# A decoder trunk on one core: new durations in the table that sets the order of the instructions

## The chip, the cores and the metric

The kernel runs on 1 core of one Trainium2 chip. The metric is the device time of one execution, in microseconds (us). TensorE does the matmuls, VectorE and ScalarE the elementwise work, GpSimd (POOL) a few small operations, and SyncE issues the loads.

## The reference

Two decoder layers are run over 256 positions of width 1024, in float32 (norms, convolutions, the mLSTM recurrence and the softmax are left out here):

```python
for layer in range(2):
    u = rmsnorm(h) @ w_in[layer]
    y = concat([mlstm(u), conv31(u), diff_attention(u)])
    h = h + y @ w_out[layer]
    c = rmsnorm(h)
    if layer % 2 == 0:
        f = (silu(c @ wg) * (c @ wu)) @ wd              # dense, 2816 wide
    else:                                               # top 2 of 8 experts, 3584 wide each
        f = sum(combine[:, e:e + 1] * ((silu(c @ wg[e]) * (c @ wu[e])) @ wd[e]) for e in range(8))
    h = h + f
    h = h + sigmoid(rmsnorm(h) @ w_gate[layer]) * (p[layer] @ w_ple[layer])
```

## The kernel before

**Weights.** Nearly all the time goes to weights that are used once. They come as tiles of 128x2048 float32, 1 MB each, into `raw` buffers (five of `rawp`, and in the expert stage four of `rawb`). ScalarE rounds a tile to fp32r as `hi` (`high`, L352), VectorE computes `lo = raw - hi` (`low`, L370), and TensorE multiplies by hi and by lo into the same PSUM tile. There are 4 hi and 3 lo buffers in the expert stage; both come free when TensorE has finished the tile (`done`, L397), the raw buffer when lo is made. So the hi of a tile waits for TensorE to be done with the tile four before it, and the lo for the tile three before it.

**Stages.** In each layer the in-projection goes by columns (pz, pm, pq, pk, pmv, pav), with the mLSTM, the convolution (z, on VectorE) and the attention (plg, ac, pya) beside it; then come the out-projection (pwo), the feed-forward part, and the gated input embedding (ppp, pgt). Layer 0 has the dense feed-forward part (pg, pu, pdn), layer 1 the experts.

**Experts.** They are taken in the pairs (0,1), (2,3), (4,5), (6,7), after the tokens that each expert got are gathered (pgx, gx) into slots: 128 ("many") for experts 0, 2 and 4, and 64 ("few") for the others. A tile of a many expert is 12 matmuls with 512 columns, one of a few expert 8, since hi and lo then share a pass and a small matmul `pht` folds them. Each expert has 7 slices f; a slice is two tiles gate (pmg), two up (pmu), two down (pmy). ScalarE and VectorE make from pmg and pmu the input of down: msl, msg, `pht` on TensorE, then mt in hi and lo form. The regular cycle of a pair is 12 tiles: pmg and pmu of the many expert, pmy of the few one, pmg and pmu of the few one, pmy of the many one. Between pairs results are scattered back (psc, added to h by VectorE) and the next tokens gathered. At the first slice of expert 2 `gate_up` (L1399) has a branch on the device at L1420, for experts with more than 64 tokens; it isn't taken here, but all engines meet at it.

**The order.** The kernel is written as one main stream (TensorE's matmuls) and side streams (generators, `side`). While the program is built, a planner keeps an estimated clock for each engine: `tick` adds an operation's estimated cost, `estimate` gives the time at which a stream's next step could begin, `best` (L205) takes the earliest, and `slot` (L212) writes what begins before TensorE's clock runs out, ahead of the next matmul group. hi and lo are such steps too, which `Feed.due` offers when a load's estimated landing (`pump`) and a buffer's release permit. What is written is the order on each engine. The costs are in `pe_cost` (L107), `act_cost` (L116), `dve_cost` (L123), `pool_cost` and in `pump` (L323). Every instruction goes through the helper `call`, so in the trace nearly all have its line, L101, and are told apart by the names of their tiles.

Of the kernel before, what the change touches and what calls it, by code (L numbers as in the profile page):

```python
# [64 lines left out]
def tile_trunk(ctx, tc, x, par, con, abias, wif, rw, pt, w1, w2, wgu, wdn, wpg, wpp, wm, gb, out):  # L65
# [38 lines left out]
    def size(*aps):  # L104
        return max(math.prod(a.shape[1:]) for a in aps if hasattr(a, "shape"))

    def pe_cost(op, a, kw):  # L107
        if op == "transpose":
            return 0.107
        if kw["rhs"].dtype == F32R:  # L110
            return size(kw["rhs"]) / 2400
        return max(size(kw["rhs"]) / 600, 0.1)

    tables = [None]

    def act_cost(op, a, kw):  # L116
        c = 0.2 + size(*a[:2]) / 1400
        if len(a) > 2 and a[2] not in (AF.Copy, AF.Square, AF.Abs) and a[2] != tables[0]:
            tables[0] = a[2]
            c += 1.28  # L120
        return c

    def dve_cost(op, a, kw):  # L123
        return (0.13 if op == "scalar_tensor_tensor" else 0.1) + size(*a[:2]) / 960

    def pool_cost(op, a, kw):
        return 0.25 if op in ("memset", "affine_select") else 0.13 + 0.166 * size(a[0])

    pe, act = Engine(nc.tensor, pe_cost), Engine(nc.scalar, act_cost)
    dve, pool = Engine(nc.vector, dve_cost), Engine(nc.gpsimd, pool_cost)  # L130
    main = Stream()
    cur = [main]
# [167 lines left out]
    class Feed:  # L300
# [14 lines left out]
        def pump(self, upto=None):  # L315
            while self.loaded < (upto or (len(seq) if self.order else first_moe)):
                which = next((w for w in "pb" if self.free[w]), None)
                if which is None:
                    return
                src = seq[self.loaded]  # L320
                if isinstance(src, tuple):
                    src = wm[(self.order[src[0]],) + src[1:]]
                self.dma = max(self.dma, self.free[which].pop(0)) + 2.65  # L323
                raw = (rawp if which == "p" else F[which]).tile([128, 2048], F32, name="raw" + which, tag="raw" + which)

                step = 1024 if self.loaded in (0, 1, first_moe, first_moe + 1, last_moe, last_moe + 1) else 2048
                for c in range(0, 2048, step):
                    nc.sync.dma_start(raw[:, c:c + step], src[:, c:c + step])
                self.raws[self.loaded] = raw, which, [self.dma + 2.0 - 1.3 * (1 - q) * (step == 1024) for q in range(2)]
                self.loaded += 1  # L330
# [1254 lines left out]
    for n in range(3 * DEPTH):  # L1585
        L, c = divmod(n, 3)
# [134 lines left out]
```

## Time and profile before

| | |
|---|---|
| three runs, us | 1435.37, 1439.47, 1432.83; median 1435.37 |
| profiled execution, us | 1433.88, span 1432.2, mean granted clock 0.986 |
| TensorE busy, us | 1379.7 (96%), 6500 instructions |
| VectorE busy, us | 1197.2 (84%), 1222 |
| ScalarE busy, us | 1045.5 (73%), 1194 |
| GpSimd busy, us | 58.2 (4%), 73 |
| HBM read | 435.39 MB, 305 GB/s over the span |

A trace is read by stage here: 0 to 345 us is layer 0 (its dense part from about 160 to 320), 345 to 513 attention and the rest of layer 1's mixing, 513 to 1388 the experts, and the end is the last scatter and the embedding. Matmuls overlap by their pipeline, so a duration in a row is longer than the distance of two starts. In a timeline row the time in brackets is what the engine stood idle just before, with what ended it.

### The profile page before, as it was taken

How to read it: one execution, taken by the hardware profiler on the slowest of the kernel's cores; microseconds unless marked ns; L12 is line 12 of the kernel's file. 1: busy time of each engine (PE TensorE's matmuls, PEld its weight loads, DVE VectorE, ACT ScalarE, POOL GpSimd, SP SyncE). 2: the span in 40 equal slices, each digit the busy share in tenths (PEclk: the TensorE clock that was granted, in tenths of full speed). 3: DMA queues.
4: the chain of work that ended last, by engine and by line, in shares of the span. 5: the costliest groups of instructions: out<-in, count | busy, mean ns of one | idle time of the engine just before them, and what ended most of it. 6: DMA issues, size and time to landing. Idle time of an engine off the chain costs nothing. (4 is left out here: it accounts for less than half of the span.)

```text
span 1432.2 us, 18251 instructions
## 1 busy us (share of the span) xinstructions
PE 1379.7 (96%) x6500; PEld 1118.2 (78%) x6500; DVE 1197.2 (84%) x1222; ACT 1045.5 (73%) x1194; POOL 58.2 (4%) x73
## 2 busy tenths in 40 slices
PE   7999999999999989999999999999999999999998
PEld 6777888888877867888878888887878887767666
DVE  5997654546899579999979999988999998999986
ACT  7766534436776577888878888886888888888875
POOL 0212000000031100000000000000000000000000
PEclk9998999999998989999999999999999999999999
DMA  9243555554440099999998999998999999999970
GB/s 361 89 147 126 206 176 195 187 183 170 145 147 30 16 402 421 420 422 420 421 417 337 420 407 417 406 388 319 413 415 408 402 402 367 418 420 422 421 310 30
DMA packets 62766, 437.66 MB, mean 306 GB/s; under 512 B 7120, under 2 KB 8016, under 8 KB 10832
## 3 DMA queue, kind: packets, MB, share of 16 engines
q1 hardware_dynamic: 62352, 435.42, 76.3%
q8 instruction: 52, 0.85, 0.2%
q0 software_dynamic: 320, 1.05, 0.2%
q14 instruction: 42, 0.34, 0.1%
HBM read 435.39 MB, written 1.05 MB: 305 GB/s over the span
## 5 line engine op out<-in xcount | busy, mean ns | idle before, releaser
L101 DVE TENSOR_TENSOR lo<-rawp,hi 128x2048 fp32r<-128x2048 f32 (+1 forms) x336 | 598.1, 1806 | 126.7 <-ACT hi L101 114.1
L101 ACT ACTIVATE hi<-rawp 128x2048 fp32r<-128x2048 f32 (+1 forms) x336 | 502.5, 1525 | 164.7 <-PE pg L101 34.9
L101 DVE TENSOR_TENSOR lo<-rawb,hi 128x2048 fp32r<-128x2048 f32 (+1 forms) x154 | 342.2, 2246 | 15.6 <-ACT hi L101 6.4
L101 ACT ACTIVATE hi<-rawb 128x2048 fp32r<-128x2048 f32 (+1 forms) x154 | 287.0, 1882 | 33.5 <-PE pmu L101 12.8
L101 PE MATMUL pmy<-hi,mt 128*128 128x512 f32 x616 | 224.1, 398 | 0.1
L101 PE MATMUL pmg<-hi,gx 128*128 128x512 f32 x616 | 220.8, 397 | 0.9 <-DVEq L1420 0.9
L101 PE MATMUL pmu<-hi,gx 128*128 128x512 f32 x616 | 219.3, 395 | 0.0
L101 PE MATMUL pmu<-lo,gx 128*128 128x512 f32 x448 | 177.6, 396 | 11.2 <-DVE lo L101 10.3
L101 PE MATMUL pmg<-lo,gx 128*128 128x512 f32 x448 | 177.4, 396 | 9.9 <-DVE lo L101 9.8
L101 PE MATMUL pmy<-lo,mt 128*128 128x512 f32 x448 | 175.6, 392 | 0.5 <-DVE lo L101 0.3
L101 PEld LDWEIGHTS pmg<-hi,gx 128*128 128x128 f32 x616 | 116.1, 189 | 25.2 <-issue 2.2
L101 PEld LDWEIGHTS pmy<-hi,mt 128*128 128x128 f32 x616 | 115.8, 188 | 23.7 <-DVE mt L101 0.7
L101 PEld LDWEIGHTS pmu<-hi,gx 128*128 128x128 f32 x616 | 115.8, 188 | 22.8 <-issue 0.2
L101 PEld LDWEIGHTS pmu<-lo,gx 128*128 128x128 f32 x448 | 84.1, 188 | 37.9 <-DVE lo L101 21.1
L101 PEld LDWEIGHTS pmg<-lo,gx 128*128 128x128 f32 x448 | 84.4, 188 | 35.1 <-DVE lo L101 18.4
L101 PEld LDWEIGHTS pmy<-lo,mt 128*128 128x128 f32 x448 | 84.2, 188 | 19.7 <-DVE lo L101 1.8
L101 PEld LDWEIGHTS pht<-conT,msg 128*128 128x128 f32 x560 | 73.0, 191 | 8.1 <-ACT msg L101 2.4
L101 PE MATMUL pht<-conT,msg 128*128 128x64 f32 x560 | 70.2, 268 | 1.5 <-ACT msg L101 1.5
L101 DVE SCALAR_TENSOR_TENSOR z<-zpad,parT,z 128x256 f32<-128x256 f32 x120 | 50.9, 479 | 0.3
L101 PE MATMUL pg<-hi,nh 128*128 128x512 f32 x96 | 37.7, 393 | 0.0
L101 PE MATMUL pg<-hi,nl 128*128 128x512 f32 x96 | 37.4, 390 | 0.0
L101 PE MATMUL pg<-lo,nh 128*128 128x512 f32 x96 | 37.4, 389 | 0.0
(299 smaller groups left out, 1873.0 us busy)
## 6 DMA issues: line engine op xcount, KB each, us to landing
rawp<-in_wm SPq DMA_DIRECT2D x184, 1024.0 KB, 8.7
rawb<-in_wm SPq DMA_DIRECT2D x148, 1024.0 KB, 8.7
rawp<-in_w SPq DMA_DIRECT2D x30, 1024.0 KB, 4.7
rawp<-in_wgu SPq DMA_DIRECT2D x22, 1024.0 KB, 4.7
rawp<-in_wdn SPq DMA_DIRECT2D x11, 1024.0 KB, 4.8
rawp<-in_wpg SPq DMA_DIRECT2D x5, 1024.0 KB, 4.7
rawp<-in_wm SPq DMA_DIRECT2D x8, 512.0 KB, 7.8
rawb<-in_wpg SPq DMA_DIRECT2D x3, 1024.0 KB, 10.3
```

The lines of the kernel that those rows point to most:

```text
L101: return fn(*args, **kw)
```

## The change

The figures for the duration of an instruction and of a load are others. A matmul with 512 columns has 0.228 us instead of 0.213; a hi of 2048 elements 1.836 instead of 1.663; a lo of 2048 2.203 instead of 2.233; a 64-column fold (`pht`) 0.2 instead of 0.107; a load of 1 MB 2.48 instead of 2.65. What is computed, the buffers and the order of the loads stay; the order in which ScalarE's, VectorE's, TensorE's and GpSimd's work is written moves.

```diff
@@ -108,20 +108,20 @@
         if op == "transpose":
             return 0.107
         if kw["rhs"].dtype == F32R:
-            return size(kw["rhs"]) / 2400
-        return max(size(kw["rhs"]) / 600, 0.1)
+            return 0.01 + size(kw["rhs"]) / 2350
+        return max(size(kw["rhs"]) / 600, 0.2 if size(kw["rhs"]) == 64 else 0.1)
 
     tables = [None]
 
     def act_cost(op, a, kw):
-        c = 0.2 + size(*a[:2]) / 1400
+        c = 0.1 + size(*a[:2]) / 1180
...
     def dve_cost(op, a, kw):
-        return (0.13 if op == "scalar_tensor_tensor" else 0.1) + size(*a[:2]) / 960
+        return (0.15 if op == "scalar_tensor_tensor" else 0.07) + size(*a[:2]) / 960
...
@@ -320,7 +320,7 @@
-                self.dma = max(self.dma, self.free[which].pop(0)) + 2.65
+                self.dma = max(self.dma, self.free[which].pop(0)) + 2.48
```

In the regular cycle, here of experts 2 and 3, ScalarE (its own queue, in order) has before:

```order
L101 ACTIVATE msl<-pmg 128x512
L101 ACTIVATE hi<-rawp 128x2048 x2
L101 ACTIVATE hi<-rawb 128x2048
L101 ACTIVATE mt<-pht 128x4x128
L101 ACTIVATE hi<-rawb 128x2048 x2
L101 ACTIVATE msg<-pmg 128x512
L101 ACTIVATE hi<-rawb 128x2048
L101 ACTIVATE msl<-pht 128x256
L101 ACTIVATE hi<-rawp 128x2048
L101 ACTIVATE msg<-pmu 128x512
```

and now:

```order
L101 ACTIVATE msl<-pmg 128x512
L101 ACTIVATE hi<-rawp 128x2048 x4
L101 ACTIVATE mt<-pht 128x4x128
L101 ACTIVATE hi<-rawb 128x2048 x2
L101 ACTIVATE msg<-pmg 128x512
L101 ACTIVATE hi<-rawb 128x2048 x2
L101 ACTIVATE msl<-pht 128x256
L101 ACTIVATE msg<-pmu 128x512
L101 ACTIVATE hi<-rawp 128x2048
L101 ACTIVATE mt<-msl 128x4x64
```

mt<-pht (the hi form of the many expert's down input) stands behind four hi instead of three, and msg<-pmu directly behind msl<-pht.

VectorE in the regular cycle, here of experts 0 and 1, has before:

```order
L101 TENSOR_TENSOR msl<-msl,pmu 128x512
L101 TENSOR_TENSOR lo<-rawb,hi 128x2048 x3
L101 TENSOR_TENSOR mt<-pht,mt 128x4x128
L101 TENSOR_TENSOR lo<-rawb,hi 128x2048
L101 TENSOR_TENSOR lo<-rawp,hi 128x2048 x2
L101 TENSOR_TENSOR msl<-msl,pht 128x256
L101 TENSOR_TENSOR lo<-rawp,hi 128x2048
L101 TENSOR_TENSOR mt<-msl,mt 128x4x64
```

and now:

```order
L101 TENSOR_TENSOR msl<-msl,pmu 128x512
L101 TENSOR_TENSOR lo<-rawb,hi 128x2048 x2
L101 TENSOR_TENSOR mt<-pht,mt 128x4x128
L101 TENSOR_TENSOR lo<-rawb,hi 128x2048 x2
L101 TENSOR_TENSOR lo<-rawp,hi 128x2048 x2
L101 TENSOR_TENSOR msl<-msl,pht 128x256
L101 TENSOR_TENSOR lo<-rawp,hi 128x2048
L101 TENSOR_TENSOR mt<-msl,mt 128x4x64
```

mt<-pht,mt (its lo form) stands behind two lo instead of three.

In experts 6 and 7, where both have 64 slots and a half cycle is six tiles, ScalarE has before:

```order
L101 ACTIVATE mt<-msl 128x4x64
L101 ACTIVATE hi<-rawp 128x2048 x3
L101 ACTIVATE msg<-pmg 128x512
L101 ACTIVATE hi<-rawb 128x2048
L101 ACTIVATE msl<-pht 128x256
L101 ACTIVATE hi<-rawb 128x2048
L101 ACTIVATE msg<-pmu 128x512
L101 ACTIVATE hi<-rawb 128x2048
L101 ACTIVATE mt<-msl 128x4x64
```

and now:

```order
L101 ACTIVATE msg<-pmg 128x512
L101 ACTIVATE hi<-rawb 128x2048 x2
L101 ACTIVATE msl<-pht 128x256
L101 ACTIVATE msg<-pmu 128x512
L101 ACTIVATE hi<-rawp 128x2048 x3
L101 ACTIVATE mt<-msl 128x4x64
L101 ACTIVATE hi<-rawp 128x2048
```

Two hi stand between msg<-pmg and msl<-pht instead of one, and three, instead of one, between msg<-pmu and the mt behind it.

At the branch of L1420 VectorE's last two lo before it move from ahead of the four h<-h,psc additions to behind them, still ahead of the branch, and TensorE's psc stands ahead of the last 24 pmu matmuls instead of behind them. In the attention stages VectorE's z steps move earlier, and the norm of the queries (yn) comes behind two hi halves of its weights.

## Rows read from the trace of the kernel before

**Rows 1.** The page: span, busy time of each engine, TensorE's busy tenths in forty slices.
```profile
span 1432.2 us, 18251 instructions
PE 1379.7 (96%) x6500; PEld 1118.2 (78%) x6500; DVE 1197.2 (84%) x1222; ACT 1045.5 (73%) x1194; POOL 58.2 (4%) x73
...
PE   7999999999999989999999999999999999999998
```

**Rows 2.** Windows: stretch, length, busy us (instructions) of PE, PEld, DVE, ACT, POOL; clock, DMA share, GB/s.
```profile
540.00:700.00 160.00, 160.00 (x755) 133.43 (x755) 154.32 (x89) 131.67 (x96) 0.00 (x0) 1.00 1.01 421
1240.00:1370.00 130.00, 120.18 (x566) 92.99 (x565) 124.32 (x72) 111.75 (x90) 0.00 (x0) 1.00 1.01 421
```

**Rows 3.** Timeline, TensorE, experts 0 and 1: first pmu matmul, five cycles apart.
```profile
550.97 0.39 PE L101 MATMUL pmu<-hi,gx 128*128 128x512 f32 x1
...
698.82 0.39 PE L101 MATMUL pmu<-hi,gx 128*128 128x512 f32 x1
```

**Rows 4.** The chain of waits, later pairs: start, length, engine, tile, count.
```profile
771.90 5.44 PE pmu L101 x24
...
892.85 5.44 PE pmu L101 x24
923.64 5.44 PE pmu L101 x24
...
996.25 5.44 PE pmu L101 x24
...
1148.54 5.44 PE pmu L101 x24
```

**Rows 5.** Timeline of one cycle of experts 2 and 3: ScalarE, VectorE, TensorE.
```profile
871.61 0.60 ACT L101 ACTIVATE mt<-pht 128x512 fp32r<-128x512 f32 x1 [2.15 <-PE pht L101]
872.11 3.71 ACT L101 ACTIVATE hi<-rawp 128x2048 fp32r<-128x2048 f32 x2
...
874.05 4.49 DVE L101 TENSOR_TENSOR lo<-rawp,hi 128x2048 fp32r<-128x2048 f32 x2 [0.81 <-ACT hi L101]
...
876.39 0.50 PE L101 MATMUL pmu<-lo,gx 128*128 128x512 f32 x1 [0.94 <-DVE lo L101]
```

**Rows 6.** Timeline of one cycle of experts 0 and 1: VectorE, and one TensorE row.
```profile
615.58 2.29 DVE L101 TENSOR_TENSOR lo<-rawp,hi 128x2048 fp32r<-128x2048 f32 x1 [0.43 <-PE pmu L101]
...
618.38 6.69 DVE L101 TENSOR_TENSOR lo<-rawb,hi 128x2048 fp32r<-128x2048 f32 x3
...
623.27 0.39 PE L101 MATMUL pmu<-hi,gx 128*128 128x512 f32 x1
...
624.99 0.69 DVE L101 TENSOR_TENSOR mt<-pht,mt 128x512 fp32r<-128x512 f32 x1
625.59 2.28 DVE L101 TENSOR_TENSOR lo<-rawb,hi 128x2048 fp32r<-128x2048 f32 x1
```

**Rows 7.** Timeline around the branch.
```profile
750.25 0.69 DVE L101 TENSOR_TENSOR h<-h,psc 128x512 f32<-128x512 f32 x1 [1.03 <-PE psc L101]
...
751.15 0.47 PE L101 MATMUL pmg<-hi,gx 128*128 128x512 f32 x1 [0.93 <-DVEq L1420]
```

**Rows 8.** VectorE's waits, 1240 to 1370 (total us, times, longest), and the timeline there.
```profile
DVE lo L101 <- ACT hi L101: 4.9, 9, 0.7
...
1310.05 0.42 DVE L101 TENSOR_TENSOR msl<-msl,pht 128x256 f32<-128x256 f32 x1
...
1320.23 0.38 ACT L101 ACTIVATE msl<-pht 128x256 f32<-128x256 f32 x1 [0.62 <-PE pht L101]
...
1324.82 0.42 DVE L101 TENSOR_TENSOR msl<-msl,pht 128x256 f32<-128x256 f32 x1
```

**Rows 9.** Windows (columns as rows 2) in the attention stages of layer 0 and layer 1.
```profile
98.00:104.00 6.00, 4.05 (x21) 2.70 (x19) 5.83 (x16) 5.17 (x18) 0.00 (x0) 1.00 0.23 61
106.00:114.00 8.00, 8.00 (x26) 6.24 (x25) 7.27 (x25) 5.96 (x26) 0.80 (x1) 0.50 0.09 35
450.00:462.00 12.00, 12.00 (x37) 9.27 (x38) 10.97 (x37) 8.57 (x35) 1.49 (x2) 0.50 0.00 0
```

## Prediction

> **What bounds the kernel now.** First I read the page's shares and its forty slices [rows 1]. TensorE is busy for 96% of the span, and its digit is 9 in nearly every slice, so only a moment in which TensorE waits, or runs at a lower clock, can be won or lost: 1432.2 less 1379.7 is 52.5 us in all. VectorE at 84% is next. The dense feed-forward part (160 to 320 us, the fifth to eighth slice and half of the ninth) has nothing but 9, and its order is the same before and after, so nothing happens there.
>
> A share of the whole span does not say which engine ends last in a stage, so I read windows of the expert stage [rows 2]. In experts 0 and 1 (540 to 700) TensorE works 160.00 of 160 us, with VectorE at 154.32 and the loads at 421 GB/s, a share of 1.01: all three are full, and TensorE ends last. In experts 6, 7 (1240 to 1370) TensorE loses 9.82 of 130 us, and VectorE is the fuller one, at 124.32.
>
> Then I measured the cycle of the expert loop. One cycle of a pair is twelve 1 MB weight tiles, and the first matmul of the same pmu tile marks its start. Five cycles of pair 0, 1 run from 550.97 to 698.82 [rows 3]: 147.85 us, or 29.57 each. The chain of waits marks the same point in the later pairs [rows 4]: 771.90 to 923.64 is 151.74 for five, with 30.79 for the last, and 996.25 to 1148.54 is 152.29. Twelve tiles are 12.58 MB, which at 421 GB/s take 29.89 us, so the loads pace nearly the same cycle.
>
> The 1.2 us by which the slow cycle is longer show in the timeline [rows 5]. ScalarE stands 2.15 us at mt<-pht, which TensorE has not yet produced, with two hi halves queued behind it; so VectorE waits 0.81 for a hi, and TensorE 0.94 for the lo made from it.
>
> **The change, part by part.** It removes and adds no operation, buffer or load. It changes what the planner believes, and so which instruction it writes next. The new figures are those of the rows: 24 matmuls in 5.44 us are 0.227 each [rows 4], for which the planner now has 0.228 instead of 0.213; three lo in 6.69 are about 2.20 each [rows 6], for which it has 2.20 instead of 2.23; two hi in 3.71 are about 1.85 [rows 5], for which it has 1.84 instead of 1.66. That the change does nothing can be left out, as the order of three engines differs. The load order on SyncE's queue is the same; a load waits for the lo that frees its buffer, and a lo that comes 0.6 later is hidden by the backlog of loads (share 1.01 in [rows 2]). Without the backlog it would cost up to those 0.6 per cycle.
>
> *Regular cycle, ScalarE.* mt<-pht moves behind four hi instead of two or three. One more hi, 1.85 us, then fills the 2.15 that ScalarE waited [rows 5], and the hi behind mt are one fewer. At most 0.3 of the wait is left there, and the two waits that came from it go. What is late next is on VectorE.
>
> *Regular cycle, VectorE.* Its mt<-pht,mt moves one lo forward. In the old order the three lo run from 618.38 to 625.07, with mt behind them [rows 6]. The new order puts mt, which costs 0.60 to the next start (624.99 to 625.59), ahead of the third, which then ends at about 625.67. TensorE needs it after eight hi matmuls and one more: 623.27 + 9 x 0.227 = 625.31. It would wait 0.36, and with the hand-over I take 0.4 per cycle; the bounds are 0 (an earlier start of the lo, since VectorE has two waits of 0.43 before them) and 0.6. The cycle becomes 29.57 + 0.40 = 29.97 in all pairs, just over the loads' 29.89. Experts 0, 1: 6 x 0.40 = **+2.4**. Experts 2, 3: 151.74 and a sixth cycle of 30.79, less 6 x 29.97 = **-2.7**. Experts 4, 5: 152.29 + 30.79 - 179.82 = **-3.2** (rounded).
>
> *The branch at L1420.* Before, VectorE makes the last addition of psc to h from 750.25, 0.03 after TensorE's last matmul, and TensorE goes on at 751.15, a wait of 0.93 [rows 7]. Now VectorE has two lo behind the h additions and ahead of the branch, and the last needs a buffer that TensorE frees with its last matmul before the branch. One lo of 2.2 and the 0.2 around it then stand where 0.93 stood: +1.5 (bounds 0 and 2.4). Behind the branch ScalarE has a hi ahead of a msg that TensorE's fold needs. A hi is 1.85 us [rows 5]; I take about half, +1.0 (bounds 0 and 1.85). Together **+2.5**.
>
> *Experts 6, 7.* Six tiles take 14.77 us, from the msl at 1310.05 to the one at 1324.82 [rows 8]. VectorE loses 4.9 us in 9 waits for a hi, 0.54 each, because ScalarE waits 0.62 at msl<-pht with a hi behind it. In the new order two hi come before msl<-pht and three behind msg<-pmu, and I find no place where a hi is late: I take 4.5 of the 4.9: **-4.5** (bounds 0 and -6, with the 9.82 that TensorE loses in the window above it).
>
> *Attention and convolution, both layers.* VectorE's z steps move earlier, and a norm there comes behind two hi halves. No row of before shows that order. The nearest rows are the stretches at half clock: 8 us and 12 us at 0.50 [rows 9], which in layer 0 follow a stretch where TensorE had worked only 4.05 of 6.00 us with VectorE full (5.83). If they went, half of 20 us is won (-10); if they came again with the idle time of 1.95 ahead of each, +14 is lost. VectorE's chain gets no shorter, so I stay near zero on the late side, as a few halves moved ahead cost part of one idle time: **+1.5**.
>
> The sum is 2.4 - 2.7 - 3.2 + 2.5 - 4.5 + 1.5 = -4.0, and against the profiled execution's own 1433.9 that gives 1429.9, told as **1430**. That execution is 1.5 us below the median of the runs shown (1435.4), so the new median may stand up to 1.5 higher.
>
> **The rivals.**
> *The lo is in time.* If the two waits of 0.43 in VectorE's row [rows 6] move with the order, the third lo is ready at 625.3 and the cycle stays at 29.57 in all three pairs. 18 cycles x 0.4 are 7.2 less: **1423**. For it: only 0.36 us is missing. Against it: those waits are for buffers that TensorE frees, and TensorE moves with them.
>
> *The loads set experts 6, 7.* Six tiles are 6.29 MB, 14.94 us at 421 GB/s [rows 2], and the cycle now takes 14.77. If the loaded tiles ahead are used up, nothing is left of the 4.5: **1434**. For it: a share of 1.01 through the whole window. Against it: the cycle already beats 14.94, and what VectorE waits for there is ScalarE's hi, behind a wait for TensorE.
> The Trainium skill, Perfetto Trace Analysis (section Roofline), puts the practical ceiling of a single active core at about 435 GB/s. By that figure six tiles need an estimated 14.46 us, and some 0.3 of each 0.54 would be left; the 421 of the window lies below it, and no run here shows more.
>
> *The half clock lasts longer, the slower end.* One mechanism in one place, between the in-projection and pwo: if VectorE's norm for the queries ends later, TensorE idles longer there, and the stretch at 0.50 comes a second time. Each stage pays the idle 1.95 and half of 8 or 12 us: 6 and 8 us [rows 9]. In one stage that gives about 1436, in both 1429.9 - 1.5 + 14 = 1442.4, and on the scale of the median **1443**. It decides if TensorE stands idle there once more, as it did ahead of the stretch of before. For it: that order changes most, and TensorE is idle there already. Against it: TensorE has pieces of pwo and norms to put there, and most z steps move ahead of time, not behind.
> The Trainium skill's TensorE: Matmul & The Clock Gate, Part 1, says that the clock is halved after TensorE has been little busy and restored once it works. The rows agree, with 1.00 in the idle stretch, 0.50 in the busy one that follows. By that rule the loss is several times the idle time itself.
>
> **How the numbers follow.** About 0.5%, here 7 us, is what a measurement of this kernel can tell from no change. The forecast has 0.45, and its own range is 1426 to 1435 from the bounds of the lo, the branch and experts 6, 7; about 0.14 of it lies under 1428. The lo in time has 0.25, the loads 0.13. The half clock has 0.17, of which 0.06 in one stage, and 0.11 in both. Faster by over 0.5% is then 0.25 + 0.14 = 0.39; slower 0.11, with 0.01 for the far end of the one-stage case: 0.12; the rest, 0.49, lies between. The range of 1420 to 1441 leaves out the both-stage case and the fast end of the first rival, where experts 6, 7 give 6 instead of 4.5.
>
> **What would show each step right or wrong.** Right: in experts 2 to 5 no wait of ScalarE at mt<-pht; a wait of TensorE of about 0.4 per cycle for the lo behind VectorE's mt, and 29.97 us between pmu starts, in experts 0, 1 too; TensorE 2 to 3 us idle at the branch; six tiles in about 14.2 in experts 6, 7 with no wait of VectorE for a hi. Wrong: cycles still over 30.5 (another wait has replaced the first); 14.9 in experts 6, 7 with waits for a raw tile (the loads); a granted clock of 0.50 for more than 20 us in the two stages. The forecast is wrong as a whole if the expert stage is not 6 to 10 us shorter while the mixing stages stay within 3 us.

## The result, and the profile after

The changed kernel takes 1442.06 us (median of 16 runs, 1439.65 to 1446.15), the kernel before 1434.32 (16 runs): a ratio of 1.0051, 95% interval 1.0043 to 1.0060. It is 8 us slower; 1430 was forecast, and the range ended at 1441. The profiled execution took 1442.0 us.

The page of the changed kernel, its first part and the slices, to be read beside [rows 1]:

```profile
span 1440.3 us, 18380 instructions
PE 1386.9 (96%) x6500; PEld 1123.4 (78%) x6500; DVE 1195.0 (83%) x1222; ACT 1047.0 (73%) x1194; POOL 52.9 (4%) x73
...
PE   7999999999999989999999999999999999999988
```

Nothing in it tells where the 8 us went: the shares are the same to a percent. The first pgx of each pair of experts (the gather) is a mark that both traces have. From such marks, in one profiled execution of each kernel:

| stretch | before, us | after, us | difference | forecast |
|---|---|---|---|---|
| start to first pgx (dense layer, both attentions, router) | 501.24 | 511.04 | +9.8 | +1.5 |
| experts 0, 1 | 219.60 | 222.85 | +3.3 | +2.4 |
| experts 2, 3, with the branch | 225.14 | 227.50 | +2.4 | -0.2 |
| experts 4, 5 | 224.88 | 221.97 | -2.9 | -3.2 |
| experts 6, 7 and the end | 261.3 | 256.9 | -4.4 | -4.5 |

**The expert loop did what was worked out.** Rows of the changed kernel's timeline, VectorE, ScalarE and TensorE in one cycle of experts 4 and 5, which answer to [rows 5, 6]:

```profile
1048.88 0.68 DVE L101 TENSOR_TENSOR msl<-msl,pmu 128x512 f32<-128x512 f32 x1
...
1052.28 0.57 ACT L101 ACTIVATE mt<-pht 128x512 fp32r<-128x512 f32 x1
...
1053.88 0.68 DVE L101 TENSOR_TENSOR mt<-pht,mt 128x512 fp32r<-128x512 f32 x1
...
1056.82 0.50 PE L101 MATMUL pmu<-lo,gx 128*128 128x512 f32 x1 [0.25 <-DVE lo L101]
...
1078.96 0.68 DVE L101 TENSOR_TENSOR msl<-msl,pmu 128x512 f32<-128x512 f32 x1
```

ScalarE's wait of 2.15 at mt<-pht is gone. VectorE's mt is ahead of the third lo, TensorE waits for it, and the cycle is 30.08 us from msl to msl: slower than the 29.57 of [rows 3], faster than the 30.79 of [rows 4]. It is 30.1 in all three pairs; 29.97 was forecast. Five cycles of experts 0 and 1 are 2.6 us longer than before (150.48 and 147.85, from msl to msl). What is left of the table's +3.3 lies ahead of the first of them (+0.8), where the changed kernel has a stretch at a mean clock of 0.57 (544 to 548), behind a wait of 1.24 us for a lo; the execution of before has 1.00 at that place.

In experts 6 and 7 six tiles take 13.88 us instead of the 14.77 of [rows 8], VectorE waiting for no hi. The timeline has VectorE's msl of two half cycles:

```profile
1279.45 0.41 DVE L101 TENSOR_TENSOR msl<-msl,pht 128x256 f32<-128x256 f32 x1
...
1293.33 0.41 DVE L101 TENSOR_TENSOR msl<-msl,pht 128x256 f32<-128x256 f32 x1
```

ScalarE's waits (total us, times, longest) from 1345 to 1395 us:

```profile
ACT hi L101 <- DMA rawp<-in_wm: 2.9, 5, 0.8
ACT hi L101 <- DMA rawb<-in_wm: 2.2, 5, 0.6
```

13.88 is less than the 14.94 that six tiles take to load at 421 GB/s. The tiles loaded ahead are used up, and at the end ScalarE waits for loads; the last three half cycles take 14.31, 16.12 and 11.84 us. In the second of them TensorE waits 1.70 us for a msg (at 1371.9), and the clock is at 0.50 from 1374 to 1376. Six half cycles in a row had won 5.4 us (88.72 before, 83.27 after); the stretch as a whole won 4.4.

**The branch** cost more than the 2.5 forecast: from the last msl<-msl,pmu of experts 0 and 1 to the second one of experts 2 and 3 it is 72.92 us before and 77.14 after, +4.2. The timeline there, beside [rows 7]:

```profile
760.41 2.29 DVE L101 TENSOR_TENSOR lo<-rawb,hi 128x2048 fp32r<-128x2048 f32 x1 [1.88 <-PE pmu L101]
...
763.13 2.29 DVE L101 TENSOR_TENSOR lo<-rawp,hi 128x2048 fp32r<-128x2048 f32 x1 [0.43 <-PE pmu L101]
...
765.62 0.52 PE L101 MATMUL pmg<-hi,gx 128*128 128x512 f32 x1 [2.36 <-DVEq L1420]
```

Two windows behind it (columns as rows 2), and one of TensorE's waits, for the msg of a fold:

```profile
766.00:768.00 2.00, 2.00 (x6) 1.60 (x5) 0.00 (x0) 0.17 (x1) 0.00 (x0) 0.50 0.98 385
768.00:770.00 2.00, 2.00 (x7) 1.56 (x6) 0.78 (x1) 1.21 (x1) 0.00 (x0) 0.67 0.82 340
```

```profile
PE pht L101 <- ACT msg L101: 1.2, 1, 1.2
```

The idle time is 2.36, as worked out (0.93 and 1.5), and the wait behind the branch 1.2 (1.0). What was left out is the clock: right after the idle time it is at 0.50, the 1.2 GHz level, for 2 us and part of the next two, which costs about 1.6.

**The 9.8 us ahead of the experts** are the surprise. Windows of both kernels between the same marks (columns as rows 2): in-projection from pm to pav, attention from pav to pg (layer 0) or to the router's prl (layer 1), router from prl up to the first expert matmul. First before:

```profile
25.07:80.70 55.63, 55.54 (x271) 43.92 (x270) 50.97 (x100) 39.39 (x61) 11.46 (x12) 1.00 0.44 165
80.70:142.21 61.51, 56.89 (x274) 45.10 (x272) 50.39 (x125) 42.74 (x114) 10.60 (x11) 0.92 0.36 130
359.19:427.94 68.75, 68.69 (x328) 54.83 (x327) 61.22 (x120) 49.08 (x82) 12.95 (x18) 0.98 0.42 148
427.94:489.94 62.00, 59.21 (x277) 46.76 (x276) 46.58 (x119) 40.08 (x113) 11.03 (x12) 0.89 0.09 31
489.94:512.97 23.03, 17.85 (x126) 16.89 (x125) 12.62 (x41) 10.30 (x23) 0.93 (x1) 0.80 0.49 185
```

and after:

```profile
25.57:82.37 56.80, 55.52 (x271) 43.86 (x270) 53.04 (x105) 39.67 (x61) 11.79 (x12) 1.00 0.44 162
82.37:147.06 64.69, 58.40 (x274) 45.46 (x272) 49.48 (x123) 43.69 (x115) 8.01 (x11) 0.92 0.35 123
364.37:434.21 69.84, 68.61 (x327) 54.74 (x326) 63.44 (x125) 49.34 (x82) 13.30 (x18) 0.98 0.41 145
434.21:498.19 63.98, 58.75 (x277) 45.97 (x276) 44.62 (x113) 39.82 (x113) 8.41 (x12) 0.92 0.09 30
498.19:523.05 24.86, 19.68 (x126) 18.71 (x125) 12.61 (x41) 10.41 (x23) 0.94 (x1) 0.74 0.47 178
```

TensorE's number of instructions is the same but for one, the length is not: +1.2, +3.2, +1.1, +2.0, +1.8. Length less PE's busy time gives the idle time: in the four stretches ahead of the router it grows by 1.2, 1.7, 1.2 and 2.4, in all 6.5 us. The clock is not the cause in the attentions (0.92 and 0.92; 0.89 and 0.92). In the router it is, where the clock falls from 0.80 to 0.74 and the idle time stays at 5.18: there is a new stretch at 0.50 from 500 us, while TensorE works. (Up to pgx the router takes 12.8 us instead of 11.3. The rest of the 9.8 is 0.5 us ahead of the first pm and 0.3 between the attention of layer 0 and the in-projection of layer 1.)

Where TensorE's idle time in the attention goes, by its waits (total us, times, longest): in each layer of the changed kernel, and before in layer 0 and in layer 1.

```profile
PE pat L101 <- DVE ac L101: 3.4, 3, 2.6
```

```profile
PE pat L101 <- DVE ac L101: 1.9, 2, 1.0
...
PE pat L101 <- DVE ac L101: 0.8, 1, 0.8
```

These waits grow by 1.5 and 2.6 us. ac is the product of one head's softmax chain: plg on TensorE, lg and nm on VectorE, the exponentials on ScalarE, ac on VectorE, pat on TensorE. Its start, layer 0, before:

```profile
85.59 0.92 PE L101 MATMUL plg<-kT,qT 64*128 64x256 f32 x4
86.43 2.89 PE L101 MATMUL pnd<-v,wt 128*128 128x65 f32 x24
...
91.36 1.01 DVE L101 TENSOR_REDUCE nm<-lg 128x2 f32<-128x512 f32 x2
```

and after:

```profile
87.16 2.79 PE L101 MATMUL pnd<-v,wt 128*128 128x65 f32 x24
89.88 1.57 PE L101 MATMUL plg<-kT,qT 64*128 64x256 f32 x8
...
95.67 1.01 DVE L101 TENSOR_REDUCE nm<-lg 128x2 f32<-128x512 f32 x2
...
107.14 0.90 PE L101 MATMUL pat<-conT,ac 128*128 128x128 f32 x3 [2.60 <-DVE ac L101]
```

The first plg has lost its place ahead of the 24 pnd (the mLSTM's read-out). Counted from the first pav (80.70 and 82.37), it starts at 7.5 instead of 4.9 us, and the first nm at 13.3 instead of 10.7: the chain starts 2.6 us late. The same two lines are swapped in layer 1.

### The profile page after: what moved, and what is told of

The parts are those of the page before. It is cut to its first block, busy times and chain, and to the rows that moved or that the text cites. A ratio compares the mean times of both kernels' runs of the same rounds, so it can differ in the third digit from the quotient of the medians.

```text
span 1440.3 us, 18380 instructions
## 1 busy us (share of the span) xinstructions
PE 1386.9 (96%) x6500; PEld 1123.4 (78%) x6500; DVE 1195.0 (83%) x1222; ACT 1047.0 (73%) x1194; POOL 52.9 (4%) x73
## 5 line engine op out<-in xcount | busy, mean ns | idle before, releaser
L101 PE MATMUL pmy<-hi,mt 128*128 128x512 f32 x616 | 227.1, 402 | 1.3 <-DVE mt L101 1.3
```

The costliest lines, as they stand in the source:

```text
L101: return fn(*args, **kw)
```

## The experiments

All are compared with the kernel before, run on the same chip; a ratio has its 95% interval.

**e1 and e2: the change by stages.** The old and the new figures stand side by side, and a flag is turned over where the experts begin, in `moe`, ahead of `gather(0)`. e2 begins with True and turns to False.

```diff
+    shown = [False]
...
-        c = 0.2 + size(*a[:2]) / 1400
+        c = 0.1 + size(*a[:2]) / 1180 if shown[0] else 0.2 + size(*a[:2]) / 1400
...
         emitted(("order",))
+        shown[0] = True
```

> New durations from the first gather of the experts on, old ones before it. Theory S (the loss lies in the order of attention, convolution and router, which came out 9.8 us later, while the experts' order gains about 1.7 net): mixing as before, about 1432.5 us, ratio 0.997 to 1.000. Rival W (the experts' new order is only good or bad together with the state in which the mixing leaves queues and loads): 1438 or more.

> The reverse: new durations up to the router, old ones from the first gather on. Theory S: about 1444 us (1434.3 + 9.8), the first msl of the experts 10 us later than before. Rival W: 1434 to 1438, since the old order of the experts would take up part of the delay in its waits.

e1: 1432.21 us, ratio 0.9982 (0.9971 to 0.9993). e2: 1446.55, ratio 1.0080 (1.0067 to 1.0094). Theory S holds: the experts' new order alone is a small gain, the order ahead of them a loss of 11.8 us, more than the change as a whole.

**e3: truer prices of small operations.**

```diff
-        c = 0.1 + size(*a[:2]) / 1180
+        c = 0.1 + size(*a[:2]) / 1180 + (0.18 if "accum_out" in kw else 0.0)
...
-        return (0.15 if op == "scalar_tensor_tensor" else 0.07) + size(*a[:2]) / 960
+        return max(0.2, (0.15 if op == "scalar_tensor_tensor" else 0.07) + size(*a[:2]) / 960)
```

> The new durations, and two more taken from the trace: ScalarE operations that also accumulate a sum cost 0.18 us more (0.50 and 0.38 in the trace for 256 and 128 elements, 0.32 and 0.21 in the changed table), and no VectorE operation costs less than 0.2 (the table has 0.07 for two elements). Theory P (the attention order is bad because the changed table prices its small operations lower still than the old one, away from the trace): the mixing stages come back to within 2 us of before, total about 1434. Rival C (the planner's order reacts to any figure, and a truer price does not bring a better order): the mixing stages stay 5 us or more behind those of before, total 1439 or more.

1445.75 us, ratio 1.0070 (1.0057 to 1.0083). Theory P falls: with figures nearer to the trace the kernel is 11.0 us slower than before. In its profiled execution, the slowest of the five (1450.35), the attentions take 66.1 and 69.3 us (before 61.5 and 62.0), and in layer 0 TensorE waits 6.6 us at once for ac:

```profile
PE pat L101 <- DVE ac L101: 6.6, 1, 6.6
```

**e5, e6, e7: one figure at a time, up to the router.** The flag of e2, with only ScalarE's, only VectorE's or only TensorE's new figure behind it.

> Before, with ScalarE's new durations alone, and only up to the router. Theory A (the loss comes with ScalarE's figure, which prices 256 and 128 elements lower while they take longer in the trace): at least 6 us behind before at the first gather, about 1441 or more. Rival C (no one figure carries it; any change of a figure gives another order of the attention, as good or bad as it falls): a shift of the mixing stages between 0 and 10 us for each of the three figures, none of them near 0 by itself while the others carry all.

> The same with VectorE's new durations alone, up to the router. Theory A: within 2 us of before (1434.8). Rival C: 3 us or more late.

> The same with TensorE's new pace for fp32r matmuls alone (0.228 instead of 0.213 for 512 columns), up to the router. Theory A: within 2 us of before, since that figure agrees with the trace. Rival C: 3 us or more late.

e5: 1432.84 us, ratio 0.9988 (0.9973 to 1.0003); e6: 1433.21, 0.9990 (0.9977 to 1.0002); e7: 1437.94, 1.0020 (1.0008 to 1.0033). Theory A falls. None carries the loss, and their sum, -1.8 - 1.4 + 3.3, is about nothing, where all new figures together cost 11.8 (e2; the figures of the small fold and of a load, which e2 has too, were not tried apart). Rival C as I had written it doesn't hold either: two of the three are near nothing.

What the slow kernels share was then looked for in TensorE's order. In the changed kernel, e2 and e3 the first plg stands behind pnd; before, and in e5, e6 and e7, ahead of it. It turns round when TensorE's and ScalarE's figures are new together, and not with TensorE's and VectorE's.

**e9, e10: two pairs of figures**, by the same flag.

> Before, with TensorE's and ScalarE's new durations together, only up to the router. In this order, as in the changed kernel's, TensorE's first plg of each layer stands behind the 24 pnd instead of ahead of them. Theory N (this place costs the loss: the attention's chain of dependent work starts 2.6 us later in each layer): at least 5 us over before, about 1440 or more, although the two figures alone gave -1.8 and +3.3. Rival C (orders differ at random, and the effects of the figures add up): 1436, +1.5.

> The same with TensorE's and VectorE's new durations. Here the first plg stays ahead of pnd in both layers. Theory N: within 4 us of before, under 1439. Rival C by sums: +1.9, about 1436.5; a loss of more than 5 would speak against theory N.

e9: 1444.83 us, ratio 1.0075 (1.0057 to 1.0092), 10.4 over before where the two figures alone add up to 1.5: as theory N has it. e10: 1439.66, 1.0038 (1.0019 to 1.0057), 5.2 over before. That misses the expectation (under 4) and is over the 5 that was to speak against theory N, though the interval, 2.7 to 8.2 us, leaves both open. In its profiled execution the attentions are 1.4 us longer than before, the rest is in-projection and router. The place of plg is thus not the whole loss.

**e11: that place set back.** In e2's kernel, the first head gets a rank ahead of pnd's (which has -0.5):

```diff
-        side(*[attn(hd) for hd in range(4)], pen=-0.3)
+        side(attn(0), pen=-0.6)
+        side(*[attn(hd) for hd in range(1, 4)], pen=-0.3)
```

> All new durations up to the router and old ones behind it (1446.6 measured), and the first head's attention stream is given a priority ahead of pnd's, so that the first plg stands ahead of pnd again. Theory N: the attention stages come back by 2 to 3 us per layer, about 1441. Rival C: the order behind that place differs anyway, and nothing is won: 1445 to 1448.

1439.88 us, ratio 1.0038 (1.0025 to 1.0050): 6.7 less than e2 (6.0 by the two ratios, as they ran on different chips), somewhat more than theory N has. In its timeline the first plg is 4.9 us behind the first pav again, and nm 10.1, with the same table and the same work:

```profile
88.46 0.92 PE L101 MATMUL plg<-kT,qT 64*128 64x256 f32 x4
89.30 2.89 PE L101 MATMUL pnd<-v,wt 128*128 128x65 f32 x24
...
93.67 1.01 DVE L101 TENSOR_REDUCE nm<-lg 128x2 f32<-128x512 f32 x2
```

The profiled execution shows where: the two attentions are 2.9 us shorter than e2's, and the router 1.6, since the half clock did not come there. But it is not TensorE's waiting that went. The two attentions (columns as rows 2), first of e2:

```profile
82.10:146.84 64.74, 58.45 (x274) 45.45 (x272) 49.48 (x123) 43.68 (x115) 8.01 (x11) 0.92 0.34 124
433.98:497.93 63.95, 58.71 (x277) 45.97 (x276) 44.63 (x113) 39.83 (x113) 8.42 (x12) 0.92 0.09 30
```

and of e11:

```profile
83.59:147.16 63.57, 57.32 (x274) 44.43 (x272) 49.51 (x123) 44.05 (x115) 9.76 (x11) 0.89 0.35 125
433.03:495.26 62.23, 55.77 (x277) 42.87 (x276) 44.44 (x113) 39.98 (x113) 10.16 (x12) 0.95 0.09 31
```

TensorE's busy time falls by 4.1 us, and its idle time grows by 1.2; its waits at pat for ac are 5.8 us instead of 6.8, with 3.0 new ones at plg for lg. The two attentions together (first pav to pg, and to prl), by one profiled execution of each:

| first plg | kernel | sum of both, us | TensorE idle in it, us |
|---|---|---|---|
| ahead of pnd | before; e5; e6; e7; e10; e11 | 123.5; 121.7; 122.1; 125.3; 124.9; 125.8 | 7.4; 6.8; 9.8; 13.7; 15.4; 12.7 |
| behind pnd | after; e2; e9; e3 | 128.7; 128.7; 128.8; 135.4 | 11.5; 11.5; 12.6; 18.0 |

In the sums the two groups don't overlap, though 4 us lie within the first between kernels that differ only in the order behind that place. In the idle time they do: e7, e10 and e11, with plg ahead of pnd, wait as long as the changed kernel or longer. Theory N holds for the time in e9 and e11 and misses it in e10, and its mechanism, that TensorE waits because the chain starts late, is not shown: in e10, with the first nm at 10.5 us as early as before, the waits at pat for ac are 6.6 us, in the changed kernel 6.8. Why the busy time is less with plg ahead was not separated. In e7 and e10 the clock has a part in it (0.94 over both attentions, in the changed kernel 0.92); in e11 it is 0.92 as well.

**e4: the branch.** In the changed kernel, psc of experts 0 and 1 waits for a name that is set when the last pmu ahead of the branch is written.

```diff
-                yield when(pe, *[(a, e) for a in ("Y", "PT") for e in es])
+                yield when(pe, *[(a, e) for a in ("Y", "PT") for e in es], *(["GO"] if es == [0, 1] else []))
...
             if (e, f) == (2, 0):
+                set_ready("GO")
```

> The changed kernel, but the scatter of experts 0 and 1 is held until the last pmu before the branch is written, so that psc covers VectorE's two lo again. Theory B (at the branch the change costs 1.4 of idle time, about 1.6 by the half clock after it and 1.2 by TensorE's wait for a msg): the wait for the branch is 0.9 instead of 2.4, no stretch at 0.50 near it, about 1438 us, 4 less than the changed kernel. Rival I (the idle time alone counts; the clock falls there anyway): 1.5 less, about 1440.5.

1438.97 us, ratio 1.0027 (1.0017 to 1.0037), 3.1 less than the changed kernel (3.4 by the two ratios): between the two theories, nearer to B. TensorE's wait is the old one, and in the windows the clock stays at 1.00:

```profile
757.87 7.03 PE L101 MATMUL psc<-my,PT 128*128 128x512 f32 x16
765.82 0.47 PE L101 MATMUL pmg<-hi,gx 128*128 128x512 f32 x1 [0.93 <-DVEq L1421]
```

```profile
764.00:766.00 2.00, 1.07 (x4) 0.27 (x3) 0.69 (x1) 0.23 (x1) 0.00 (x0) 1.00 0.49 197
766.00:768.00 2.00, 2.00 (x11) 1.61 (x11) 0.74 (x2) 0.61 (x2) 0.00 (x0) 1.00 0.05 16
```

From the msl ahead of the branch to the second one behind it are 72.65 us, 4.5 less than in the changed kernel. The clock stays up at the branch in e8 and e12 too, which have this edit; e1, which has the changed order there without it, has a stretch at half clock behind the branch like the changed kernel. Its profiled execution reached the experts 1.8 us later than the changed kernel's, with the same order up to there; that is the spread of single executions. Part of it is a stretch at half clock in the in-projection (0.65 and 0.50 from 54 to 58 us) where the changed kernel's execution has 1.00.

**e8: the lo that mt was put ahead of.** New figures in the experts alone (e1), psc as in e4, and VectorE's mt held until one more lo has been written.

```diff
-                yield from splits((T[:, :, 0], T[:, :, 1], p, None))
+                yield act
+                act.activation(T[:, :, 0], p, AF.Copy)
+                yield when(dve, ("LO", feed.lows + 1))
+                dve.tensor_tensor(T[:, :, 1], p, T[:, :, 0].bitcast(F32), op=ALU.subtract)
...
+            self.lows += 1
+            set_ready(("LO", self.lows))
             dve.tensor_tensor(lo, r, hi.bitcast(F32), op=ALU.subtract)
```

> New durations in the experts alone, psc behind pmu at the branch, and in the regular cycle VectorE's mt held until three lo instead of two are written. Theory L (the new cycle of 30.10 us is 29.57 and TensorE's wait for the lo that mt was put ahead of): 29.57 while loaded tiles are ahead, and then the loads' 29.89; 18 cycles are 4 to 9 us less, and with 3 us at the branch 1421 to 1426. Rival D (the loads bound it: what is won in the cycles is lost in waits for raw tiles up to the end of experts 6 and 7): 1428 to 1430, with waits of ScalarE's hi for a load late in each pair and in experts 6, 7.

1418.93 us, ratio 0.9892 (0.9873 to 0.9911): 15.7 us faster than before, more than expected. The cycle of experts 4 and 5 in the timeline, and below it a window in experts 2 and 3:

```profile
1028.80 0.68 DVE L101 TENSOR_TENSOR msl<-msl,pmu 128x512 f32<-128x512 f32 x1
...
1058.34 0.68 DVE L101 TENSOR_TENSOR msl<-msl,pmu 128x512 f32<-128x512 f32 x1
```

```profile
830.00:930.00 100.00, 100.00 (x473) 83.57 (x472) 95.97 (x54) 84.18 (x61) 0.00 (x0) 1.00 1.01 421
```

29.54 us, with TensorE busy 100 of 100. One lo ahead of mt is thus worth 0.5 us per cycle. The stretches from pgx to pgx are 219.8, 219.9 and 219.5 us, where before they were 219.6, 225.1 and 224.9: what the old order lost from pair to pair is gone. Rival D falls for these pairs, since 29.57 holds although the loads need 29.89; in experts 6 and 7 it shows as in the changed kernel, with ScalarE waiting for loads in the last 50 us.

**e12: the changed kernel with all three places put right.**

> The changed kernel with all its durations, and the three places put right together: the first plg ahead of pnd, psc behind the last pmu at the branch, three lo ahead of mt in the regular cycle. If the three places are what the change loses and act apart from each other: the 1418.9 of the kernel with the last two and the old mixing, and the 5.4 that the mixing still lost with plg first, about 1424. If they are not apart (the mixing's delay is taken up by the loads, which then run further ahead): 1419 to 1421. If the experts' gain depended on the old mixing: 1430 or more.

1423.02 us, ratio 0.9920 (0.9907 to 0.9934). That is within 1.3 us of the 1424 expected if the three places act apart from each other. e8, which keeps the old figures up to the router, is the fastest of all: the new table is the better one in the experts (e1) and the worse one ahead of them (e2).

## Why the prediction was wrong

*The failed step is the one on attention and convolution, priced at +1.5.* It measured +9.8, with the router, and by itself turns the -4.0 of the sum into a loss. I had looked there for VectorE's order (z, the norm) and the clock, and bounded the cost by the stretches at half clock. The slower rival stood in the right place with the wrong mechanism, and that its 1443 is near the 1442 measured is luck: the stretch at 0.50 did not come a second time in either attention (the stretches' mean clock is 0.92 after). What the runs show in its place: the order ahead of the experts by itself costs 11.8 us (e2); TensorE's and ScalarE's figures together bring nearly as much (e9, 10.4) and TensorE's and VectorE's 5.2 (e10), where no figure alone costs more than 3.3; and setting one place of TensorE's own order back, the first plg ahead of the 24 pnd, gives 6 to 7 us of it back (e11). I had not followed that order through the chain of plg, nm, ac and pat. "VectorE's chain gets no shorter" was true and beside the point: the chain started 2.6 us later. Whether the late start is what costs the time stays open, since e11 starts early again and TensorE waits there no less.

Of the 9.8 us the attentions are 5.2, of which 4.1 are longer waits of TensorE for ac; e11 gives 2.9 of the 5.2 back, while the planner writes another order behind it; where the other 2.3 lie in that order was not separated. Both in-projections are 1.1 to 1.2 us longer, where TensorE waits 0.7 us at pqt, put down to a hi, and 0.5 for a lo in layer 0, and 0.9 for a cc and 0.4 for a qk in layer 1; that was read, not tried. The router's 1.8 us are its new half-clock stretch. It comes in the changed kernel, e2 and e4, which have one order up to there, and in e10, and not in e9, e11 and e12, so it does not hang on plg; in the executions of e3 and e6 the clock is 0.60 from prl to pgx. What it hangs on stays open.

*The branch* was +2.5 and measured +4.2. The two terms were right, 1.4 and 1.2; the clock after the idle time, about 1.6, was put at nothing (e4 shows it gone with the idle time). The Trainium skill, TensorE: Matmul & The Clock Gate, Part 1, says that idling brings the half rate; the trace agrees, with 0.50 behind an idle time of 2.36 and 1.00 throughout behind one of 0.93. I had used this rule for the attention only, and it belonged here as well, as a risk: a wait of 2.07 us in the trace of before (for a lo, up to 531.6) is followed by 1.00.

*The regular cycle* was right in mechanism and nearly in size: 0.53 instead of 0.40 per cycle, 30.10 instead of 29.97. Experts 4 and 5 came to -2.9 for -3.2; experts 0 and 1 to +3.3 for +2.4, of which five cycles are 2.6. e8 shows the mechanism, since the wait and the 0.5 us go when the lo is put back.

*Experts 6 and 7* came out at -4.4 for -4.5, by two errors that cancel, which is luck: the half cycle is 13.88 instead of 14.2, and the rival on the loads came true for the last 50 us. The Trainium skill, Perfetto Trace Analysis, section Roofline, has the ceiling at about 435 GB/s; the trace agrees, the windows of 100 us and more staying at 421, and what let the half cycle run faster than that is the store of loaded tiles.

That the change would do what it says held too, for the large operations. For the small ones it does not: the trace has 0.50 us for an exponential of 256 elements with its sum, the new table 0.32, the old one 0.38. e3, with prices near the trace, is no faster, so truer prices don't mend it. Two readings of the prediction were loose: three lo in 6.69 us are 2.23 each, and 2.20 only from start to start, and 3.26 was told as 3.2. Neither moves the sum by more than 0.1.

## What to carry to other kernels

A list scheduler with truer durations does not write a faster order for that reason alone: it starts what can start first and does not know which chain ends last, so a small change of a figure can swap two entries, and the swap can cost several us (e11, e8). When a table of costs changes, compare the orders at the head of each dependent chain, on every engine, and hold the two or three places that matter by an explicit rule. Then look in the trace whether the rule won what it was written for: e11 won time, but not the waits. Here three such rules gave 11 us (e12), where the new table without them lost 8.

## What the runs showed of the hardware that was not expected

A wait of 2.36 us at the branch was followed by more than 2 us at half clock, one of 0.93 at the same place by none. The length of one wait does not decide it alone: 1.70 us at 1371.9 was followed by 0.50, and 2.07 us at 531.6 of the kernel before by 1.00. Nor does more waiting mean more half clock: layer 1's attention has a mean clock of 1.00 in e7, with 6.7 us of idle time, and 0.89 before, with 2.8. And TensorE's clock fell to 0.50 in the router while TensorE worked 2.00 of 2.00 us:

```profile
498.00:500.00 2.00, 2.00 (x20) 2.00 (x18) 0.25 (x1) 2.00 (x9) 0.00 (x0) 0.92 0.00 0
500.00:502.00 2.00, 2.00 (x11) 2.00 (x11) 1.56 (x8) 1.23 (x4) 0.31 (x1) 0.50 0.00 0
```

The work ahead of it is sixteen matmuls prl with 8 columns; the twelve filler matmuls behind them (busy, 256 columns) take 2.91 us, before 1.67. Ahead of it lies one idle time of 0.56 us (496 to 498) and another of 0.55 at 489. Before, two idle times of 0.55 at the same places of the program (in 480 to 482 and 488 to 490), and the same prl matmuls, are followed by 1.00.

Where the clock falls also differs between executions of one order (54 to 58 us in e4 and in the changed kernel), and their times go with it: of the ten executions of e6 the fastest took 1430.8 us at a mean clock of 0.992, the slowest 1439.7 at 0.984. A stage's time in one profiled execution can thus be off by some us, where the medians of the kernel before, in five sets of runs, lie between 1434.0 and 1434.8.
